# Three blocks for even tokens ahead of the odd ones, and the merges' weights transposed later and stored from another queue

## The chip, the cores and the metric

The kernel runs on one core of one Trainium2 chip. A core has TensorE (PE, with its weight loads shown apart as PEld), VectorE (DVE), ScalarE (ACT), GpSimd (POOL) and SyncE (SP). Each has its own queue of instructions and works it off in order; they wait for one another by semaphores. Transfers between the core's memory and DRAM are issued from such a queue too, here nearly all from SP's and some from GpSimd's, and run on 16 DMA engines. The metric is the time of one execution on the device, in microseconds.

## The reference

The kernel computes one hybrid decoder block over 1024 tokens of width 1024 in float32. In short:

```
h = rms_norm(x, g_pre_mix);  z = h @ w_in
q, k, v, glu_in, z_ga, z_gc = split(z)
# attention: 3 groups (dilations 1, 4, 16) of 8 heads of 64, a banded window of 128 steps
o_g, lse_g = dilated_group_attention(q_g, k_g, v_g, bias_g, window_g, dilation_g)
alpha  = softmax(stack(lse_g), axis=groups)
y_attn = (sum_g alpha_g * o_g) @ w_attn_out
# convolution: gated unit -> causal depthwise conv of 31 taps -> layer norm -> swish -> projection
u = silu(layer_norm(causal_depthwise_conv(u_in * sigmoid(gate)) + b_dw))
y_conv = u @ w_conv_out + b_conv_out
merged = sigmoid(z_ga) * y_attn + sigmoid(z_gc) * y_conv
x = x + rms_norm(merged @ w_mix_out)
x = x + rms_norm(swiglu_ffn(rms_norm(x)))
```

Two places matter here. One is `u @ w_conv_out`, the convolution's projection. The other is `alpha`, by which the three groups' attention outputs are merged, head by head and token by token.

## The kernel before, in words

A product of float32 matrices is done as three matmuls of rounded parts: every operand is split into a high part (a cast on ACT) and a low part (the remainder, a subtraction on DVE or GpSimd). A unit of such a product is a block of 128 output columns for 512 tokens: eight steps of 128 in depth, three matmuls each (lines 305, 307, 309), 24 matmuls into one PSUM bank.

The program writes the order of every engine's instructions out by hand. The main loop issues matmuls. After each step of depth (three matmuls) `tick` is called, which advances background generators: a generator's `yield n` lets n further ticks pass before it goes on. After each single matmul `beat` is called, which advances attention (the generator `fine`) at a set rate of steps per matmul. So "some steps later" means some ticks later, and where an instruction stands in its engine's queue follows from the ticks, not from time.

The part around the change is the stage in which attention's last steps run beside the convolution's projection. At its start stands the last gate projection; then come 16 units of the convolution's projection: 8 blocks of output columns n, each for the even tokens (hf = 0) and for the odd tokens (hf = 1). Per unit:

- `B.weights(co[n])`, called at the unit for even tokens, makes sure that the weights of block n are split, loads those of block n + 2 from SP's queue (line 177) and queues the split of block n + 1, in two halves, one each few ticks (line 188 on ACT, 189 on DVE). A load of the gate values of block n + 1 follows on SP (line 1569).
- `B.unit` does the 24 matmuls. Its right-hand operands come from `conv_split`, a background generator that loads the normalised convolution output and splits it in 16 pieces, first eight for even tokens, then eight for odd ones (line 1242 on ACT, 1243 on DVE). When a unit asks for a piece that is not there yet, the generator is advanced at that point.
- Line 1586 on DVE adds the bias and multiplies by the gate, which frees the PSUM bank; the result is stored by SP some ticks later (line 1588).

The units stand in the order (n, hf) = (0, even), (1, even), (0, odd), (1, odd), (2, even), (2, odd), (3, even) and so on.

Attention itself does scores (line 1049, with the bias and a running minimum on DVE, line 1052), exponentials (1062 on ACT), transposes of the probabilities (1087, copied by ACT on 1094 and split by DVE on 1095), and the products with the values (1122), whose outputs DVE copies (1142).

For each of four head pairs (hp = 0 to 3) a `merge` runs as a background generator when that pair's last group is done. It computes the merge weights alpha on DVE (lines 1170 to 1177, with one exponential on ACT, 1172) in one small tile `mrg`, of which there is a single buffer for all four merges. PE transposes the weights (1183), ACT copies them from PSUM (1184), SP stores them to DRAM (1188). From there they are loaded back spread over partitions (`spread`, line 1158), beside the attention outputs (line 1197), and DVE multiplies and adds (1211, 1215, 1220, 1225, 1230). The result is split (195, 196) and is the operand of attention's output projection, which comes after the 16 units.

While attention runs, PSUM has two banks for units (tag g), two for scores, two for transposes, two for attention's outputs. Once all four merges have done their transpose (`B.weighed == 4`) the next unit to begin switches to six banks for units.

Of the kernel before, what the change touches and what calls it, by code (L numbers as in the profile page):

```python
# [62 lines left out]
class Build:  # L63
# [1098 lines left out]
    def merge(self, hp, st, last):  # L1162

        nc = self.nc
        yield 2
        t = self.tiny(128, "mrg", 1)
        m, r = (t[:, i * 16:(i + 1) * 16].rearrange("p (u e) -> p u e", u=8) for i in range(2))
        w = t[:, 32:80].rearrange("p (g u e) -> p g u e", g=3, u=8)
        low, tot = st[:, :, :, 0:2], st[:, :, :, 2:4]
        nc.vector.tensor_reduce(m, low.rearrange("p g u e -> p u e g"), AX.X, OP.min)  # L1170
        nc.vector.tensor_tensor(w, low, m.unsqueeze(1).to_broadcast([128, 3, 8, 2]), op=OP.subtract)
        nc.scalar.activation(t[:, 32:80], t[:, 32:80], AF.Exp, scale=-1.0)
        yield 2
        nc.vector.tensor_tensor(tot, tot, w, op=OP.mult)
        nc.vector.tensor_reduce(m, tot.rearrange("p g u e -> p u e g"), AX.X, OP.add)
        nc.vector.reciprocal(r, m)
        nc.vector.tensor_tensor(t[:, 80:].rearrange("p (g e u) -> p g u e", g=3, e=2).rearrange("p g u e -> p g u e"), w,
                                r.unsqueeze(1).to_broadcast([128, 3, 8, 2]), op=OP.mult)
        yield 1
        m = r = w = low = tot = None  # L1180
        yield 3
        ps = self.bank("t")
        nc.tensor.transpose(ps[0:48, :128], t[:, 80:], self.ident)
        nc.scalar.copy(t[0:48], ps[0:48, :128])
        ps = None
        self.weighed += 1
        yield 1
        nc.sync.dma_start(self.d_w[hp].rearrange("f (u p) -> (f u) p", u=8), t[0:48])
        t = None
        yield 4  # L1190

        while not self.ending or hp > self.turn:
            yield 0

        def load(g):
            y = self.slot()
            nc.sync.dma_start(y, self.d_att[g, hp])
            return y

        y = load(0)  # L1200
        yield 1
        x = self.spread(hp, 0)
        yield 1
        z = load(1)
        yield 1
        w = self.spread(hp, 1)
        yield 7
        self.turn += hp == 0
        while self.fine is not None or hp > self.done:
            yield 0  # L1210
        nc.vector.tensor_tensor(y, y, x, op=OP.mult)
        x = None
        x = self.spread(hp, 2)
        yield 1
        nc.vector.tensor_tensor(z, z, w, op=OP.mult)
        w = None
        w = load(2) if last is None else last
        last = None
        yield 1
        nc.vector.tensor_tensor(y, y, z, op=OP.add)  # L1220
        z = None
        self.turn += hp > 0
        yield 9
        self.done += 1
        nc.vector.tensor_tensor(w, w, x, op=OP.mult)
        x = None
        yield 2

        z = self.slot()
        nc.vector.tensor_tensor(z.rearrange("p (m c) -> p c m", c=8), *(a.rearrange("p (c m) -> p c m", c=8) for a in (y, w)),  # L1230
                                op=OP.add)
        y = w = None
        yield 2
        self.OT[hp] = self.both(z)
# [166 lines left out]
def build(ctx, tc, aps):  # L1401
    B = Build(ctx, tc, aps)
    nc = B.nc
# [150 lines left out]
    def conv_rhs(hf):  # L1554
        def at(kt):
            while len(B.cop[hf]) <= kt:
                next(cs[0][0])
            x = B.cop[hf][kt]
            return x[:, :H], x[:, H:]
        return at  # L1560
# [3 lines left out]
    def gate_load(d, late=0):  # L1564
        c = B.slot()
        if late:
            B.later(late, lambda: nc.sync.dma_start(c, d))
        else:
            nc.sync.dma_start(c, d)
        return c  # L1570
# [1 line left out]
    nxt = gate_load(B.d_gc[0], 1)  # L1572
    ws = {}

    for n, hf in [(0, 0), (1, 0), (0, 1), (1, 1)] + [(n, hf) for n in range(2, 8) for hf in range(2)]:
        if hf == 0:
            ws[n] = B.weights(co[n])
            mg[n] = nxt
            nxt = gate_load(B.d_gc[n + 1]) if n < 7 else (gate_load(B.d_ga[0]), gate_load(B.d_gc[0]))
        if B.tags["g"] == 2 and B.weighed == 4:  # L1580
            B.banks(g=6, s=2)
        ps = B.unit(ws[n], conv_rhs(hf), KT)
        c = mg[n].rearrange("p (m e) -> p e m", e=2)[:, hf]
        if n >= 8 - LATE - EARLY:
            nc.scalar.activation(c, c, AF.Sigmoid)
        nc.vector.scalar_tensor_tensor(c, ps, B.col(C_BCO + n), c, op0=OP.add, op1=OP.mult)
        if hf:
            B.later(9, lambda n=n: nc.sync.dma_start(B.d_gc[n], mg.pop(n)))
            c = None
            del ws[n]  # L1590
# [210 lines left out]
    for j in range(PLAIN, FT):  # L1801
        s = [None, None]
        p, odd = divmod(j, 2)
# [105 lines left out]
    for i in range(7):  # L1909
# [12 lines left out]
        n = NP - LAST if i == 6 else NP  # L1922
# [112 lines left out]
```

## Time and profile before

| | |
|---|---|
| median of 3 runs | 1714.13 us (1712.32 to 1714.29) |
| profiled execution | 1711.05 us |
| its span in the trace | 1709.1 us |
| PE, DVE, ACT, POOL busy | 99%, 73%, 46%, 28% |
| granted TensorE clock | 0.999 |

The profile is of one execution. The span runs from the first to the last instruction, and the execution's own time is some 2 us longer. Busy time of an engine is the sum of its instructions' durations. Matmuls overlap one another, so that a matmul of 512 columns has a duration of 0.39 us, while in an undisturbed row of them one starts every 0.227 us. In a view of instructions in order, the first number is the start in us from the span's start, the second the duration; a bracket at the end of a row gives the idle time of the engine before it and the instruction that ended it. In a view of waits the numbers are the total in us, the times, and the longest. In a view of transfers, KB are those of one and the last number is the median time from issue to landing.

### The profile page before, as it was taken

What the parts mean: (1) busy time and instruction counts of PE and PEld (TensorE: products, weight loads), DVE (VectorE), ACT (ScalarE), POOL (GpSimd) and SP (SyncE); (2) the same over time, 40 slices, a digit from 0 to 9 for tenths busy, and PEclk for the clock granted to TensorE, in tenths of its full rate; (3) what the DMA queues carried; (4) which work ended last, traced back from release to release, by engine and by line L of the source; (5) the groups of instructions that cost most, each with busy time, mean ns of one, the idle gap of its engine ahead of it and who ended that gap; (6) DMA issues with size and microseconds to landing.
All of it is one profiled execution on the core that took longest, in us unless ns stands there. A gap on an engine that the chain in (4) does not pass through costs nothing.

```text
span 1709.1 us, 24547 instructions
## 1 busy us (share of the span) xinstructions
PE 1692.4 (99%) x8758; PEld 1437.4 (84%) x8758; DVE 1251.2 (73%) x2214; ACT 790.1 (46%) x1550; POOL 474.5 (28%) x383
## 2 busy tenths in 40 slices
PE   8999999999999999999999999999999999999998
PEld 7788888888888999999878888888888888888886
DVE  6789988888998667677885855775566556677686
ACT  6344344434444576677722436633333333354463
POOL 0017777887886124544300210000000000000000
PEclk9999999999999999999999999999999999999999
DMA  4352433455668887878998722123222322494234
GB/s 166 103 185 87 148 124 129 155 195 174 173 166 204 249 261 211 233 200 238 296 275 285 265 74 99 68 99 124 93 92 105 118 93 92 145 375 146 100 135 154
DMA packets 162422, 283.43 MB, mean 166 GB/s; under 512 B 47249, under 2 KB 78796, under 8 KB 162300
## 3 DMA queue, kind: packets, MB, share of 16 engines
q1 hardware_dynamic: 160204, 275.98, 50.8%
q0 software_dynamic: 1808, 5.61, 0.9%
q8 instruction: 69, 1.13, 0.3%
q14 instruction: 53, 0.43, 0.1%
q10 hardware_dynamic: 288, 0.27, 0.0%
HBM read 191.10 MB, written 95.42 MB: 168 GB/s over the span
## 4 chain that ended last, share of the span: by engine, by line
PE 95%; ACT 1%; issue 1%; DVE 1%; POOL 1%; DMA 1%; SPq 0%; DVEq 0%; ACTq 0%; POOLq 0%
PE p L321 16%; PE p L323 16%; PE p L322 16%; PE p L1919 12%; PE p L1648 5%; PE p L305 5%; PE p L307 5%; PE p L309 5%; PE p L1122 3%; PE p L948 2%; PE p L950 2%; PE p L952 2%; PE p L1049 2%; PE p L556 2%; PE p L1087 2%
## 5 line engine op out<-in xcount | busy, mean ns | idle before, releaser
L321 PE MATMUL p<-b,b 128*128 128x512 f32 x1204 | 468.6, 389 | 0.3 <-ACT c L340 0.3
L323 PE MATMUL p<-b,b 128*128 128x512 f32 x1204 | 468.4, 389 | 0.0
L322 PE MATMUL p<-b,b 128*128 128x512 f32 x1204 | 468.4, 389 | 0.0
L321 PEld LDWEIGHTS p<-b,b 128*128 128x128 f32 x1204 | 226.0, 188 | 47.8 <-ACT c L340 0.7
L322 PEld LDWEIGHTS p<-b,b 128*128 128x128 f32 x1204 | 226.0, 188 | 47.1
L323 PEld LDWEIGHTS p<-b,b 128*128 128x128 f32 x1204 | 226.0, 188 | 47.0
L1919 PE MATMUL p<-b,b 128*128 128x512 f32 x924 | 209.6, 389 | 0.0
L1919 PEld LDWEIGHTS p<-b,b 128*128 128x128 f32 x924 | 173.4, 188 | 36.0
L686 DVE SCALAR_TENSOR_TENSOR p<-b,par,p 128x511 f32<-128x511 f32 (+14 forms) x232 | 163.5, 739 | 0.0
L305 PE MATMUL p<-b,b 128*128 128x512 f32 x368 | 146.7, 399 | 1.3 <-ACT b L1242 1.2
L307 PE MATMUL p<-b,b 128*128 128x512 f32 x368 | 145.6, 396 | 0.0
L309 PE MATMUL p<-b,b 128*128 128x512 f32 x368 | 145.6, 396 | 0.0
L195 ACT CAST b<-d 128x1024 fp32r<-128x1024 f32 x86 | 90.4, 1051 | 105.1 <-POOL d L216 55.1
L196 POOL TENSOR_TENSOR b<-d,b 128x1024 fp32r<-128x1024 f32 x44 | 106.8, 2428 | 79.8 <-ACT b L195 72.4
L196 DVE TENSOR_TENSOR b<-d,b 128x1024 fp32r<-128x1024 f32 x42 | 51.3, 1222 | 101.0 <-ACT b L195 101.0
L948 PE MATMUL p<-b,b 128*128 128x256 f32 x384 | 112.8, 294 | 0.0
L952 PE MATMUL p<-b,b 128*128 128x256 f32 x384 | 112.2, 292 | 0.0
L950 PE MATMUL p<-b,b 128*128 128x256 f32 x384 | 112.2, 292 | 0.0
L1243 DVE TENSOR_TENSOR b<-b,b 128x512 fp32r<-128x512 f32 x133 | 91.7, 693 | 22.0 <-ACT b L1242 20.2
L1242 ACT CAST b<-b 128x512 fp32r<-128x512 f32 x133 | 82.1, 619 | 46.8 <-PE p L1919 18.1
L1648 PE MATMUL p<-b,b 128*128 128x512 f32 x384 | 89.4, 391 | 0.0
L195 ACT CAST b<-b 128x1024 fp32r<-128x1024 f32 x47 | 49.4, 1052 | 80.8 <-POOL b L223 37.2
(234 smaller groups left out, 3035.3 us busy)
## 6 DMA issues: line engine op xcount, KB each, us to landing
b<-w_in SPq DMA_DIRECT2D x30, 512.0 KB, 4.9
dk<-c SPq DMA_DIRECT2D x48, 256.0 KB, 2.9
dq<-c SPq DMA_DIRECT2D x48, 256.0 KB, 3.5
b<-dq SPq DMA_DIRECT2D x48, 256.0 KB, 4.3
b<-dk SPq DMA_DIRECT2D x48, 256.0 KB, 8.1
b<-w_fi SPq DMA_DIRECT2D x24, 512.0 KB, 4.8
d<-w_in SPq DMA_DIRECT2D x23, 512.0 KB, 4.8
dqS<-c SPq DMA_DIRECT2D x44, 256.0 KB, 2.2
```

What stands on the lines that cost most here:

```text
L196: self.wsplit.tensor_tensor(lo, x, f(hi), op=OP.subtract)
L305: nc.tensor.matmul(ps, hi[:, s], a, start=kt == 0, stop=False)
L307: nc.tensor.matmul(ps, hi[:, s], b, start=False, stop=False)
L309: nc.tensor.matmul(ps, lo[:, s], a, start=False, stop=kt == nk - 1)
L321: nc.tensor.matmul(ps, hi[:, s], a, start=first and kt == 0, stop=False, skip_group_check=True)
L322: nc.tensor.matmul(ps, hi[:, s], b, start=False, stop=False, skip_group_check=True)
L323: nc.tensor.matmul(ps, lo[:, s], a, start=False, stop=kt == 3, skip_group_check=True)
L686: nc.vector.scalar_tensor_tensor(A[i][:, j:], src[i][:, :H - j], w[i], A[i][:, j:], op0=OP.mult, op1=OP.add)
L948: nc.tensor.matmul(o, a, hi[:, s], start=kt == 0, stop=False)
L950: nc.tensor.matmul(o, a, lo[:, s], start=False, stop=False)
L1648: nc.tensor.matmul(banks[tt][nh], st, wt[:, nh * H:(nh + 1) * H], start=bool(kt == 0 and a), stop=bool(kt == KT - 1 and b))
L1919: nc.tensor.matmul(acc[t], x, y, start=first and e == 0, stop=last and e == 2, skip_group_check=True)
```

## The change

Three edits, all in the stage described above.

The units of the convolution's projection now stand in the order (0, even), (1, even), (2, even), (0, odd), (1, odd), (2, odd), (3, even), (3, odd) and so on. What is called at a unit for even tokens moves with it: the load of block 4's weights, the load of block 3's gate values and the split of block 3's weights now stand at the third unit instead of the fifth.

In each merge, PE's transpose comes five ticks after the weights' last step instead of three; in the last merge (hp = 3) eight. Everything behind it in that merge is moved by as much.

The transposed weights are stored from GpSimd's queue instead of SP's.

In PE's order, the first two transposes move behind some 26 other instructions, the third behind 11, the fourth behind 15 matmuls, which is out of the unit (2, odd) and into (3, even). The number of instructions on PE, ACT and DVE is the same.

```diff
@@ merge(self, hp, st, last)
         yield 1
         m = r = w = low = tot = None
-        yield 3
+        yield 5 + 3 * (hp > 2)
         ps = self.bank("t")
         nc.tensor.transpose(ps[0:48, :128], t[:, 80:], self.ident)
         nc.scalar.copy(t[0:48], ps[0:48, :128])
         ps = None
         self.weighed += 1
         yield 1
-        nc.sync.dma_start(self.d_w[hp].rearrange("f (u p) -> (f u) p", u=8), t[0:48])
+        nc.gpsimd.dma_start(self.d_w[hp].rearrange("f (u p) -> (f u) p", u=8), t[0:48])
         t = None
         yield 4
@@ build(ctx, tc, aps)
-    for n, hf in [(0, 0), (1, 0), (0, 1), (1, 1)] + [(n, hf) for n in range(2, 8) for hf in range(2)]:
+    for n, hf in [(n, hf) for hf in range(2) for n in range(3)] + [(n, hf) for n in range(3, 8) for hf in range(2)]:
         if hf == 0:
             ws[n] = B.weights(co[n])
             mg[n] = nxt
```

## The prediction

> **What bounds the kernel now.** I read the page first: the busy shares and the chain that ended last.
>
> ```profile
> span 1709.1 us, 24547 instructions
> PE 1692.4 (99%) x8758; PEld 1437.4 (84%) x8758; DVE 1251.2 (73%) x2214; ACT 790.1 (46%) x1550; POOL 474.5 (28%) x383
> PE 95%; ACT 1%; issue 1%; DVE 1%; POOL 1%; DMA 1%; SPq 0%; DVEq 0%; ACTq 0%; POOLq 0%
> ```
>
> TensorE is busy 1692.4 of 1709.1 us, so the whole kernel has 16.7 us without it, and an edit that neither adds nor removes a matmul can win only from that. Next, the view of waits for PE alone, and the busy time by stretches around the edited code (start and end of a stretch, its length, then busy time and instructions of PE, PEld, DVE, ACT, POOL, clock, DMA share, GB/s).
>
> ```profile
> PE p L305 <- ACT b L1242: 1.2, 1, 1.2
> PE p L1183 <- DVE mrg L1177: 1.2, 1, 1.2
> 841.50:854.10 12.60, 11.20 (x80) 8.98 (x79) 9.38 (x36) 8.46 (x31) 2.12 (x4) 1.00 1.05 240
> 868.50:875.50 7.00, 5.78 (x26) 4.46 (x25) 5.99 (x12) 1.54 (x4) 0.00 (x0) 1.00 0.34 105
> ```
>
> Two of PE's few waits lie on lines that the change moves. The first is the convolution's first block for odd tokens waiting for its own operands (L1242 is the rounding half of a split, L1243 the remainder). The second is the last merge's transpose (L1183) waiting for its weights (L1177), with PE's later matmuls queued behind it. The DMA share of 0.34 in the second stretch, where the first has 1.05, shows another thing: SP is standing still there.
>
> **Stall one, in PE's own rows.** Matmuls overlap, so I price a stall by the distance between starts.
>
> ```profile
> 829.72 0.48 PE L305 MATMUL p<-b,b 128*128 128x512 f32 x1
> ...
> 834.76 0.58 PE L1122 MATMUL p<-c,b 128*66 128x128 f32 x3
> ...
> 840.04 0.34 PE L1122 MATMUL p<-c,b 128*66 128x128 f32 x3
> ...
> 841.19 0.39 PE L305 MATMUL p<-b,b 128*128 128x512 f32 x1
> 841.42 0.38 PE L1087 MATMUL p<-ident,c 128*128 128x128 f32 x2
> 841.55 0.48 PE L307 MATMUL p<-b,b 128*128 128x512 f32 x1
> ...
> 849.24 0.34 PE L1122 MATMUL p<-c,b 128*66 128x128 f32 x3
> 849.68 0.50 PE L305 MATMUL p<-b,b 128*128 128x512 f32 x1
> ...
> 850.98 0.38 PE L1087 MATMUL p<-ident,c 128*128 128x128 f32 x2
> 852.60 0.49 PE L305 MATMUL p<-b,b 128*128 128x512 f32 x1 [1.25 <-ACT b L1242]
> 852.93 0.34 PE L1122 MATMUL p<-c,b 128*66 128x128 f32 x3
> 853.33 0.50 PE L307 MATMUL p<-b,b 128*128 128x512 f32 x1
> 854.13 0.40 PE L305 MATMUL p<-b,b 128*128 128x512 f32 x1
> ```
>
> 841.19 starts block 0 for odd tokens, 854.13 the next. A transpose pair is normally followed after 0.13 us (841.42 to 841.55); here after 1.62 (850.98 to 852.60): 1.49 lost. The L1122 group takes 0.16 (0.34 with an overlap of 0.18) and is here followed after 0.44 (849.24) and 0.40 (852.93), against some 0.18: 0.26 and 0.22 lost. Together 2.0 us. A cruder price: this block lasted 12.94 (841.19 to 854.13), the one before it 11.47 (829.72 to 841.19): 1.5. I take 2.0, with 1.5 as the lower end.
>
> In the change, block 2 for even tokens stands in this place and block 0 for odd tokens starts one block later. The last split on ACT begins at
>
> ```profile
> 851.93 0.62 ACT L1242 CAST b<-b 128x512 fp32r<-128x512 f32 x1
> ```
>
> and its remainder is there when PE's L307 at 853.33 takes it. It is paced by the same ticks in the new order, and the earliest that the last operand is used is then seven eighths into a block that begins near 852, that is about 860. Stall one goes whole: **-2.0**.
>
> **What takes its place.** Weights of block 3 are now split during this block instead of during the fifth: two halves, each an ACT cast (L188) and a DVE subtraction (L189), in among the attention's exponentials and copies. DVE had 9.38 of 12.60 there; 1.2 more is about 10.6 in some 11: tight. The nearest case is the block from 829.72, which carried block 2's halves: there one L1122 group was stretched to 0.58 (834.76) against 0.34 (840.04). So between 0 and 0.25, and I take **+0.15**, nearer the upper end because DVE is no emptier here. The weights must also be there:
>
> ```profile
> 833.48 0.43 SPq L177 DMA_DIRECT2D b<-w_co  x1
> DMA to landing us min/median/max: 8.0/9.8/11.6
> ```
>
> Block 3's load is issued at 833.48, in its old place on SP, so it lands at 843.3 (841.5 to 845.1); the first L188 now stands on ACT at about 844.4. The median clears it by 1.1 us, the slowest misses it by 0.7. An attention copy has about a microsecond before its L1122 group needs it, so even this costs a few tenths.
>
> On SP the load of block 4 and a gate load move ahead of one spread of the first merge and the statistics loads: 1 MB earlier by some 14 us and three more buffers held meanwhile. Those spreads are used only after attention ends (about 863), so this is priced at nothing; if that cover goes, DVE's merge steps wait, and what they feed is priced below.
>
> **Stall two, from store to transpose.** The chain view and then DVE's, PE's rows.
>
> ```profile
> 862.40 5.86 DMA dw<-mrg
> ```
>
> ```profile
> 868.38 0.23 DVE L1170 TENSOR_REDUCE mrg<-stat 128x16 f32<-128x48 f32 x1 [0.93 <-DMA dw<-mrg]
> 868.64 0.21 DVE L1171 TENSOR_TENSOR mrg<-stat,mrg 128x48 f32<-128x48 f32 x1
> 869.72 0.69 DVE L189 TENSOR_TENSOR b<-b,b 128x512 fp32r<-128x512 f32 x1 [0.87 <-ACT b L188]
> 870.33 1.22 DVE L1220 TENSOR_TENSOR b<-b,b 128x1024 f32<-128x1024 f32 x1
> ...
> 872.25 0.24 DVE L1177 TENSOR_TENSOR mrg<-mrg 128x48 f32<-128x48 f32 x1
> 872.38 0.74 DVE L1586 SCALAR_TENSOR_TENSOR b<-p,par,b 128x512 f32<-128x512 f32 x1
> ```
>
> ```profile
> 861.76 0.27 PE L1183 MATMUL p<-ident,mrg 128*48 128x128 f32 x1
> ...
> 863.52 0.40 PE L309 MATMUL p<-b,b 128*128 128x512 f32 x1
> ...
> 871.03 0.39 PE L309 MATMUL p<-b,b 128*128 128x512 f32 x1
> 872.64 0.27 PE L1183 MATMUL p<-ident,mrg 128*48 128x128 f32 x1 [1.22 <-DVE mrg L1177]
> ...
> 875.52 0.39 PE L305 MATMUL p<-b,b 128*128 128x512 f32 x1
> ...
> 929.92 0.39 PE L305 MATMUL p<-b,b 128*128 128x512 f32 x1
> ```
>
> The merges share one small tile, so merge 3 may not write it (L1170) until merge 2's store has read it: 5.86 us in a full DMA stage. DVE then does L1171, a weight half, L1220 and the reciprocal steps; L1177 ends at 872.49, PE starts at 872.64, where 871.26 was due: **1.4 us** lost.
>
> In the change merge 2's transpose comes 11 PE instructions later, behind the matmul at 863.52, so near 863.75; with stall one gone, near 861.9. Transpose to issue took 0.64 us on SP's way (861.76 to 862.40); the same puts GpSimd's issue at 862.5 to 862.6, hardly later than before. Merge 3's transpose moves 15 matmuls on, into the next block (block 3, even), one step in. That block starts at 875.52 - 1.85 - 1.4 = 872.3, the transpose is due at 873.0.
>
> Landing on GpSimd's queue has no row for this store. Bounds: the nearest stores from that queue, 512 KB in 2.9 to 7.6, and 16 KB in small pieces in up to 7.8.
>
> ```profile
> DMA to landing us min/median/max: 2.9/4.9/7.6
> dst<-stat POOLq DMA_DIRECT2D x2, 16.0 KB, 7.8
> ```
>
> I take 5, the large store's median, because this store has 512-byte rows and not 16-byte pieces: landed at 867.6. From L1170 to the end of L1586 DVE took 4.74 (868.38 to 873.12), of which 1.48 were the weight half (868.85 to 870.33) that has moved to the third block. So L1177 ends 2.5 and L1586 3.3 after landing: 870.1 and 870.9. The transpose due at 873.0 no longer waits: **-1.4**.
>
> There is a new deadline. PE's bank set changes from two to six output banks only when all four merges are transposed, looked at when a block begins; before, that was block 3 even, now it is block 3 odd. So block 3 even must reuse the bank that the L1586 above frees, by 872.3. It is free at 870.9: 1.4 us of room, cost nothing; with 7.8 to land it is 1.4 late.
>
> On GpSimd nothing waits behind the last two stores, since its next instruction is far off; the first two fall where GpSimd, 28% busy over the span, has nothing ahead but another small store. On SP the wait of merge 3's store, with a datt load, a weight load and a gate load queued behind it, is gone.
>
> ```profile
> 920.03 0.95 POOL L189 TENSOR_TENSOR b<-b,b 128x256 fp32r<-128x256 f32 x1 [75.06 <-ACT b L188]
> 915.08 1.23 DVE L196 TENSOR_TENSOR b<-b,b 128x1024 fp32r<-128x1024 f32 x1 [0.66 <-ACT b L195]
> ```
>
> Later on, attention's output projection starts at 929.92 and its last operand is split by 916.31 (915.08 + 1.23): 13.6 us of room, from which the gain takes 3 and merge 3's later steps at most 3.4 (15 matmuls of 0.227). No new wait.
>
> **Sum.** -2.0 + 0.15 - 1.4 = -3.25 us. The profiled execution took 1711.05 us (span 1709.1), so 1707.8; it stood 3.1 below the median of the three runs, 1714.13 (1712.32 to 1714.29), which makes 1710.9, 0.19% less. What this kernel's measurement tells from no change is about 0.2%, 3.4 us, so the forecast lies on the border.
>
> **Rivals.** *A: both stalls go*, gain 2.1 to 4.3 (1.5 - 0.25 + 0.9 to the full 3.5 plus scatter): 1710.9, chance 0.64, of which I put 0.34 beyond 0.2% and 0.30 within.
>
> *B: the store lands late, and the bank takes the transpose's place.* Over 6.4 us from issue to landing the block at 872.3 waits; at 7.8, for 1.4 us: gain 1.85, 1712.3. For it: the small store's 7.8. Against: it is in 16-byte pieces. The Trainium skill, "DMA: Bandwidth & Descriptors", section "Issuing engines are not separate DMA queues", speaks against the change here: DMAs of all engines share the same 16 DMA engines, and another issuing engine saves only the time to issue. By that rule the store would still take the 5.86 of the row, land at 868.5 and free the bank at 871.8, 0.5 before it is due: the same sum, with a third of the room. No row here shows one store from both queues. Chance 0.12, within 0.2%.
>
> *C: slower.* Block 3's weight half waits on ACT for its load, with the attention's exponentials and copies queued behind it, and these hold PE. Each microsecond beyond about one of room costs one. To lose the gain and 3.4 us more it needs to land 6.7 later than 845.4, 18.6 after its issue, where the slowest row has 11.6. For it: DMA share 1.05 in this stage, and 1 MB newly ahead on the rings. There it gives 1717.5, and at 20 us 1719. Chance 0.12, also for what else a tight third block may do.
>
> *D: the waits only move* (the splits for odd tokens are late again a block on, or merge 3's chain follows its transpose): 1714.1, chance 0.04. Against it speak the 8 us and 2.9 us of room above.
>
> *E: more than forecast*, 4.3 to 6: SP's freed time fills the stretch with the 0.34 share, and small losses elsewhere go too: 1709. Chance 0.08; against it PE was already full from 875.5 on.
>
> Faster by over 0.2%: 0.34 + 0.08 = 0.42. Within: 0.30 + 0.12 + 0.04 = 0.46. Slower: 0.12. A alone spans 1709.8 to 1712.0; with B, D, part of E and the scatter of the runs (1 us each way) the range is 1708.8 to 1714.5; it leaves out C and half of E.
>
> **What would show it.** Right: no PE wait on L1242 between 840 and 865, none on L1177; the two gaps of 1.62 and 1.61 gone; block 3 even starting near 872.3; SP moving between 867 and 873. Wrong: PE's wait on L1586 at block 3 even (B), ACT's L188 waiting for the weight load near 844 (C), L1242 on PE's list again (D).

## The result, and the profile after

The changed kernel is slower: 1717.75 us median of 7 runs (1714.78 to 1720.12), against 1712.32 (1710.68 to 1717.15) for the kernel before run beside it, a ratio of 1.0028 with a 95% interval of [1.0015, 1.0041] (taken over all runs; the two medians alone give 1.0032). Its profiled execution took 1718.57 us, 7.5 more than the one before. The page of the kernel after, its first lines and the chain that ended last:

```profile
span 1716.6 us, 24557 instructions
PE 1694.1 (99%) x8758; PEld 1438.3 (84%) x8758; DVE 1251.2 (73%) x2214; ACT 789.6 (46%) x1550; POOL 476.9 (28%) x387
PE 52%; issue 2%; DMA 2%; DVE 1%; ACT 0%; POOL 0%; DVEq 0%; SPq 0%; ACTq 0%; POOLq 0%
```

PE has the same 8758 matmuls; its busy time rose by 1.7 us (1692.4 to 1694.1), so some matmuls ran slower, and the other 5.8 us of the longer span are PE standing still. Where it stands is told by the view of waits for PE:

```profile
PE p L1122 <- ACT c L1094: 5.2, 1, 5.2
PE p L1049 <- DMA b<-dk: 1.4, 1, 1.4
```

The two waits that the change was forecast to remove, on L1242 and on L1177, are gone from the list. A single wait of 5.2 us has come in their place, on a line that the change does not touch: attention's product with the values (L1122), waiting for the copied probabilities (L1094). Its surroundings in time order, first GpSimd and PE:

```profile
747.33 0.61 POOL L887 CAST b<-b 64x512 fp32r<-64x512 f32 x1
747.89 0.54 POOL L1188 DMA_DIRECT2D dw<-mrg  x1
...
751.08 0.28 PE L950 MATMUL p<-b,b 128*128 128x256 f32 x1
756.54 1.20 PE L1122 MATMUL p<-c,b 128*66 128x256 f32 x3 [5.18 <-ACT c L1094]
757.54 0.41 PE L952 MATMUL p<-b,b 128*128 128x256 f32 x1
757.76 0.41 PE L948 MATMUL p<-b,b 128*128 128x256 f32 x1
...
760.21 0.29 PE L950 MATMUL p<-b,b 128*128 128x256 f32 x1
```

then DVE and ACT of the same stretch:

```profile
749.09 0.09 DVE L1052 DVE_READ_ACCUMULATOR2_ANT stat<- 128x1 f32 x1
755.22 0.22 DVE L1170 TENSOR_REDUCE mrg<-stat 128x16 f32<-128x48 f32 x1 [6.05 <-issue]
...
755.77 0.24 ACT L1172 ACTIVATE mrg<-mrg 128x48 f32<-128x48 f32 x1 [8.11 <-DVE mrg L1171]
755.92 0.57 ACT L1094 CAST c<-p 128x512 fp32r<-128x512 f32 x1
```

and the same spot before (transposition, store and the next merge's first instruction, with the store's landing from the view of transfers), followed by the landing after:

```profile
742.19 0.27 PE L1183 MATMUL p<-ident,mrg 128*48 128x128 f32 x1
...
742.86 0.32 SPq L1188 DMA_DIRECT2D dw<-mrg  x1
...
748.84 0.22 DVE L1170 TENSOR_REDUCE mrg<-stat 128x16 f32<-128x48 f32 x1
...
dw<-mrg SPq DMA_DIRECT2D x1, 24.0 KB, 1.9
```

```profile
dw<-mrg POOLq DMA_DIRECT2D x1, 24.0 KB, 7.3
```

Read together: merge 1 begins 6.65 us after merge 0's transpose (742.19 to 748.84 before), in the same tile. Before, merge 0's store had read the tile at 744.8 (742.86 + 1.9), 4.1 us before L1170 came. After, the store is issued 5.03 us later than before (747.89 against 742.86) and takes 7.3 us to land instead of 1.9: done at 755.2, 10.4 us later. That is 6.3 more than the 4.1 of room, and L1170 begins at 755.22 with DVE idle for 6.05 ahead of it. The profile says "issue" there, since it names no releaser; the time of the landing names it. ACT's exponential L1172 needs L1171, and the copy L1094 that PE wants is queued right behind L1172. So the chain runs from store to DVE to ACT to PE, and attention, which has nothing to do with the merge, waits in three queues.

Why the store goes late and lands late is told by the rows of GpSimd and SP. Before, GpSimd works off eight casts of keys in a row, with attention's store among them, and SP issues the loads of the next queries and keys (2 MB) only behind the merge's store:

```profile
742.05 0.61 POOL L886 CAST b<-b 64x512 fp32r<-64x512 f32 x1
...
744.62 0.56 POOL L1149 DMA_DIRECT2D datt<-d  x1
...
747.24 0.61 POOL L887 CAST b<-b 64x512 fp32r<-64x512 f32 x1
```

```profile
744.25 0.58 SPq L870 DMA_DIRECT2D b<-dq  x1
...
747.22 2.60 SPq L877 DMA_DIRECT2D b<-dk  x4
```

After, the merge's store stands behind those casts on GpSimd, and SP, no longer held by it, issues the same loads some three microseconds sooner, nearly all ahead of it:

```profile
740.89 0.68 SPq L870 DMA_DIRECT2D b<-dq  x1
...
744.51 3.81 SPq L877 DMA_DIRECT2D b<-dk  x4
```

So the two landings do not differ by the queue alone. The DMA share was 0.51 in the 1.9 us of the store before (742.86 to 744.76); after, it was 1.08 from 747 to 748, and 0.99 or more in every microsecond until 753.

The stall costs more than its 5.2 us. By stretches around it (busy time and instructions of PE, PEld, DVE, ACT, POOL, then the granted clock, DMA share, GB/s), the kernel after:

```profile
752.00:754.00 2.00, 0.00 (x0) 0.00 (x0) 0.00 (x0) 0.00 (x0) 0.00 (x0) 0.80 0.98 307
...
758.00:759.00 1.00, 1.00 (x7) 1.00 (x7) 0.96 (x3) 0.00 (x0) 0.70 (x1) 0.50 0.00 0
...
760.00:761.00 1.00, 1.00 (x11) 1.00 (x10) 0.95 (x3) 0.44 (x3) 0.00 (x0) 0.99 0.00 0
```

The granted clock fell during the stall (a mean of 0.80 from 752 to 754), stayed at 0.50 and came back at 760, some 3.5 us after PE began again; the matmuls of 256 columns start every 0.22 us there (757.54 to 757.76), where 0.12 is usual. By PE's starts, the stall lost 5.34 us (5.46 from 751.08 to 756.54, less the usual 0.12). The instructions behind it took 3.67 us (756.54 to 760.21), and the same ones 1.89 before (751.13 to 753.02), so another 1.8 were lost: 7.1 together. The wait for keys (L1049, 1.4 us) is the only other new loss above half a microsecond.

### The profile page after: what moved, and what is told of

It reads as the page before. It is cut to its first block, busy times and chain, and to the rows that moved or that the text cites. A ratio compares the mean times of both kernels' runs of the same rounds, so it can differ in the third digit from the quotient of the medians.

```text
span 1716.6 us, 24557 instructions
## 1 busy us (share of the span) xinstructions
PE 1694.1 (99%) x8758; PEld 1438.3 (84%) x8758; DVE 1251.2 (73%) x2214; ACT 789.6 (46%) x1550; POOL 476.9 (28%) x387
## 4 chain that ended last, share of the span: by engine, by line
PE 52%; issue 2%; DMA 2%; DVE 1%; ACT 0%; POOL 0%; DVEq 0%; SPq 0%; ACTq 0%; POOLq 0%
PE p L1919 12%; PE p L321 7%; PE p L322 7%; PE p L323 7%; PE p L1648 5%; PE p L305 3%; PE p L309 3%; PE p L307 3%; PE p L1122 1%; PE p L1049 1%; DMA b<-w_co 1%; PE p L1087 1%; DMA dgc<-b 0%; DMA b<-dact 0%; PE p L952 0%
## 5 line engine op out<-in xcount | busy, mean ns | idle before, releaser
L1242 ACT CAST b<-b 128x512 fp32r<-128x512 f32 x133 | 82.1, 619 | 48.1 <-PE p L1919 18.3
L1122 PE MATMUL p<-c,b 128*66 128x128 f32 (+1 forms) x620 | 87.2, 242 | 6.3 <-ACT c L1094 5.2
```

## The experiments

Theory one: the loss is merge 0's store, which goes late from GpSimd's queue and lands late, while merge 1 has to wait for it because all merges share one tile. Its rivals: two, the new order of the blocks costs more than it wins; three, GpSimd's own time for issuing, or its packets among the others, slow everything down. The first four kernels were run side by side with the kernel before (median 1713.53 us, 27 runs), the last four too, on another chip (1714.38 us, 27 runs); each ratio is against the kernel before beside it.

**Stores back on SP.** The changed kernel with one word undone:

```diff
-        nc.gpsimd.dma_start(self.d_w[hp]....., t[0:48])
+        nc.sync.dma_start(self.d_w[hp]....., t[0:48])
```

> The changed kernel with the stores of the merges' weights back on SP's queue; block order and delays as changed. Theory one (the store lands late on GpSimd's queue, and the one tile of the merges makes DVE wait for it in the second merge): that wait of 6 us on L1170 near 749 shrinks below 1.5 us, since SP's store landed in 1.9 us there, and the kernel gains 5 to 9 us on the changed one, so it ends 1 to 4 us below the kernel before. Rival two (the new order of blocks, with weights split and loaded earlier, costs the time): it stays 4 to 5 us above the kernel before.

Measured: 1710.97 us, ratio 0.9985 [0.9974, 0.9997]. L1170 begins at 749.00 with no wait, and the 5.2 us are gone. The queue is what turns the gain into a loss. What is left of the old second stall has moved, as rows of DVE and PE show:

```profile
872.02 0.23 DVE L1170 TENSOR_REDUCE mrg<-stat 128x16 f32<-128x48 f32 x1 [4.76 <-DMA dw<-mrg]
874.46 0.74 DVE L1586 SCALAR_TENSOR_TENSOR b<-p,par,b 128x512 f32<-128x512 f32 x1
...
875.25 0.50 PE L305 MATMUL p<-b,b 128*128 128x512 f32 x1 [0.61 <-DVE b L1586]
876.05 0.27 PE L1183 MATMUL p<-ident,mrg 128*48 128x128 f32 x1
```

Merge 2's store, issued by SP at 864.78, holds L1170 until 872.02; the transpose no longer waits, but the bank that L1586 frees does, for 0.61 us.

**GpSimd's queue, each store from a place of its own.** The changed kernel, with the copy out of PSUM put into unused columns of another tile:

```diff
-        nc.scalar.copy(t[0:48], ps[0:48, :128])
+        t = None
+        s = self.par[0:48, hp % 2 * 128:hp % 2 * 128 + 128]
+        nc.scalar.copy(s, ps[0:48, :128])
...
-        nc.gpsimd.dma_start(self.d_w[hp]....., t[0:48])
+        nc.gpsimd.dma_start(self.d_w[hp]....., s)
```

> The changed kernel, all three edits kept and the stores on GpSimd's queue, but the transposed weights are copied from PSUM into columns of the parameter tile that are no longer used, two places by turns, so that no store is read from the merges' tile. Theory one: no DVE wait for the store is left, the 5.3 us on PE and the slow matmuls behind it go, and the kernel ends 3 to 5 us below the kernel before, at a ratio of 0.997 to 0.999. Rival three (GpSimd's own time on issuing the stores, or the stores' packets, hold up attention): the wait goes but PE still stands for some us near 751, and it stays 3 to 5 us above.

Measured: 1709.82 us, ratio 0.9982 [0.9973, 0.9991]. GpSimd's and DVE's rows, and the transfer:

```profile
747.90 0.53 POOL L1190 DMA_DIRECT2D dw<-par  x1
...
749.11 0.22 DVE L1170 TENSOR_REDUCE mrg<-stat 128x16 f32<-128x48 f32 x1
...
865.95 0.22 DVE L1170 TENSOR_REDUCE mrg<-stat 128x16 f32<-128x48 f32 x1
...
dw<-par POOLq DMA_DIRECT2D x1, 24.0 KB, 6.3
```

The first store is issued just as late as in the changed kernel (747.90 against 747.89), from the same queue, and lands at 754.2; L1170 has long gone by then (749.11), and nobody waits. So GpSimd's time and packets cost nothing that can be measured: rival three falls. A late landing costs only because the tile is needed again.

**The block order alone.** The kernel before with the one line of the loop:

```diff
-    for n, hf in [(0, 0), (1, 0), (0, 1), (1, 1)] + [(n, hf) for n in range(2, 8) for hf in range(2)]:
+    for n, hf in [(n, hf) for hf in range(2) for n in range(3)] + [(n, hf) for n in range(3, 8) for hf in range(2)]:
```

> The kernel before with the new order of blocks alone. Theory one: the first stall (2.0 us, on L1242) goes and nothing takes its place but 0.2 to 0.4; the second stall, on L1177, shrinks from 1.4 to between 0 and 1.4, since a half of block 3's split has left its chain: 1.5 to 3.5 us below the kernel before. Rival two: 4 to 5 us above it, with PE waiting in the third block.

Measured: 1712.11 us, ratio 0.9988 [0.9979, 0.9997]: rival two falls, the order wins. The first stall is gone; the second, which was expected to shrink, grew. Its rows:

```profile
869.50 0.23 DVE L1170 TENSOR_REDUCE mrg<-stat 128x16 f32<-128x48 f32 x1 [3.79 <-DMA dw<-mrg]
...
872.19 0.27 PE L1183 MATMUL p<-ident,mrg 128*48 128x128 f32 x1 [1.94 <-DVE mrg L1177]
...
873.46 0.62 PE L309 MATMUL p<-b,b 128*128 128x512 f32 x1
...
876.86 0.40 PE L307 MATMUL p<-b,b 128*128 128x512 f32 x1
```

Issued by SP at 861.26, the store lets L1170 go only at 869.50. PE waits 1.94 us, and from 873.46 to 876.86 eight matmuls of 512 columns take 3.40 us, 0.425 each instead of 0.227, another 1.6 us.

**The queue alone.** The kernel before with the one word, at its old place in the ticks:

```diff
-        nc.sync.dma_start(self.d_w[hp]....., t[0:48])
+        nc.gpsimd.dma_start(self.d_w[hp]....., t[0:48])
```

> The kernel before with GpSimd's queue for the stores alone. Theory one: the first merge's store is issued near 748, behind GpSimd's copies, and lands 4 to 7 us later, so L1170 of the second merge waits 3 to 6 us, PE nearly as long, and the last merge's transpose is no earlier than before: 4 to 8 us above the kernel before. Rival two: within 1.5 us of it.

Measured: 1721.33 us, ratio 1.0051 [1.0039, 1.0064]. GpSimd and DVE:

```profile
748.35 0.53 POOL L1188 DMA_DIRECT2D dw<-mrg  x1
...
755.60 0.22 DVE L1170 TENSOR_REDUCE mrg<-stat 128x16 f32<-128x48 f32 x1 [6.15 <-DMA dw<-mrg]
```

Here the releaser is named. Merge 0 is transposed at 742.72, and yet its store goes at 748.35, behind six casts of keys (L886, L887) and attention's store: the old early place in the ticks buys nothing, because GpSimd's queue sets the time. The one word alone is worse than the whole change, and at the upper edge of what was expected (7.8 us by the medians, 8.7 by the ratio): it has nearly the same wait (5.1 us), the stall on L1242 is still there with 1.2 us, a wait for keys (L1049) takes 1.9, and the granted clock is halved behind all three (last section).

**The later transposes alone.** The kernel before with the one `yield`:

```diff
-        yield 3
+        yield 5 + 3 * (hp > 2)
```

> The kernel before with the later transposes alone: stores on SP, blocks in their old order. It computes the whole reference. Theory one (the loss is the late landing of merge 0's store on GpSimd's queue, with merge 1 right behind it in the one tile): no wait at merge 1, since SP's store there landed in 1.9 us. Stall one stays (1.25 us of PE waiting for L1242, 2.0 in all). Stall two goes or shrinks, because merge 3's transpose is due some four steps later: between 0 and -1.4, ratio 0.9990 to 1.0002. If the later transposes by themselves cost something in the first two merges, which the first four runs do not exclude, the ratio is above 1.0005 and PE's lost time near 751 is over 1 us.

Measured: 1712.66 us, ratio 0.9995 [0.9984, 1.0006], no difference that can be told. L1170 of merge 1 starts at 749.84 without a wait. The first stall stays, the second is gone (the last transpose, at 879.03, has no wait), and this profiled execution has a wait for keys, and a halved clock soon after it, that the one of the kernel before has not:

```profile
PE p L1049 <- DMA b<-dk: 1.4, 1, 1.4
PE p L305 <- ACT b L1242: 1.2, 1, 1.2
```

**Only the last two stores from GpSimd's queue.** The changed kernel, the first two merges' stores on SP:

```diff
-        nc.gpsimd.dma_start(self.d_w[hp]....., t[0:48])
+        (nc.gpsimd if hp > 1 else nc.sync).dma_start(self.d_w[hp]....., t[0:48])
```

> The changed kernel, with only the last two merges' stores on GpSimd's queue and the first two on SP. It computes the whole reference. Theory one: PE's 5 us wait near 751 and the half-speed matmuls behind it go, and the two stalls of the kernel before are gone as forecast, so 2 to 3.5 us under the kernel before, ratio 0.9980 to 0.9990; what is left is a short wait at merge 3 of under 0.5 us for merge 2's store. If the loss was spread over all four stores, the ratio stays above 1.0000.

Measured: 1710.90 us, ratio 0.9982 [0.9970, 0.9993]. PE's waits in the edited part are a short one for the bank and a 0.9 at L1049:

```profile
PE p L1049 <- issue: 0.9, 1, 0.9
...
PE p L305 <- DVE b L1586: 0.3, 1, 0.3
```

So the first two stores carry the whole loss, and by the rows of the changed kernel merge 0's alone, since nobody waits for merge 1's (merge 2's L1170 starts at 859.77 without a wait): with them, 1.0028; without them, 0.9982. That is 0.46%, 7.9 us of 1714, where PE's rows gave 7.1.

**The order, with stores on SP from their own place.** The old delays, the new order, and the store as in the second experiment, on SP:

```diff
+        s = self.par[0:48, hp % 2 * 128:hp % 2 * 128 + 128]
+        nc.scalar.copy(s, ps[0:48, :128])
...
+        nc.sync.dma_start(self.d_w[hp]....., s)
...
+    for n, hf in [(n, hf) for hf in range(2) for n in range(3)] + [(n, hf) for n in range(3, 8) for hf in range(2)]:
```

> The new block order, the old delays, stores on SP, but each store reads a place of its own (columns of another tile) so that the next merge need not wait for it. It computes the whole reference. Theory one's second half (one tile for all merges): the wait of L1170 for the store goes, and with it the 1.9 us that PE's transpose waited in the order-alone run and the half-speed matmuls behind it. What is left of that wait is DVE's weight half and L1220 ahead of the reciprocal steps: 0 to 0.7 us. Ratio 0.9970 to 0.9982 against the kernel before. If the transpose waited for DVE's other work and not for the store, the wait stays above 1 us and the ratio is 0.9985 or more.

Measured: 1709.69 us, ratio 0.9972 [0.9962, 0.9983], faster than both kernels. DVE and PE at the last merge:

```profile
865.19 0.22 DVE L1170 TENSOR_REDUCE mrg<-stat 128x16 f32<-128x48 f32 x1
...
867.49 0.25 DVE L1177 TENSOR_TENSOR mrg<-mrg 128x48 f32<-128x48 f32 x1
...
869.66 0.27 PE L1183 MATMUL p<-ident,mrg 128*48 128x128 f32 x1
```

L1177 ends 1.9 us before PE transposes, without any later transpose and without GpSimd's queue. The second stall was the tile, not DVE's other work.

**The changed kernel, on SP from own places.** As the one before, with the new delays too:

```diff
+        yield 5 + 3 * (hp > 2)
```

> The changed kernel with stores on SP and from a place of their own. It computes the whole reference. Theory one: neither queue nor tile makes anyone wait, the bank wait of the SP run (0.6 us at L305 for L1586) goes as well, so 0.5 to 1 us under that run: ratio 0.9972 to 0.9983. If the queue still mattered once the tile is free, it would differ from the run with own places on GpSimd's queue (0.9982) by more than 0.001; theory one expects less.

Measured: 1709.48 us, ratio 0.9974 [0.9962, 0.9985]. It cannot be told from the one before, so the later transposes are worth nothing that these runs can tell once the tile is free; nor, with certainty, from the same kernel on GpSimd's queue (0.9982 [0.9973, 0.9991]): the difference of 0.0008 is within both intervals.

## Why the prediction was wrong

The forecast was 1710.9 us, 0.19% less than before, in a range up to 1714.5; the result is 0.28% more.

**The step that failed** is the one that costs the first two merges' stores at nothing: "the first two fall where GpSimd, 28% busy over the span, has nothing ahead but another small store". Four things in it were wrong. GpSimd's share of the whole span says nothing of that place: the rows of the kernel before show eight casts of 0.61 us there (742.05 to 747.85), and attention's store among them is of 512 KB, not small. After, three of these casts begin behind the transpose, and the store goes 2.4 us after it (745.52 to 747.89) where SP took 0.67. The landing was 7.3 us; the prediction had asked for a landing on that queue only for merge 2's store, and had allowed 5 to 7.8 there. It saw that SP is freed where merge 3's store waited, but not that the same happens at merge 0, where the freed SP fills the DMA engines just ahead of the store. And it had named the rule that a merge may not write the tile before the store has read it, and applied it to merges 2 and 3 alone. Merge 1 follows merge 0 by 6.65 us, as closely as merge 3 follows merge 2 (transpose at 861.76, L1170 at 868.38). Before, the 1.9 us landing on SP left 4.1 us of room, so no wait was to be seen at merge 1, and the prediction looked for the change's cost only where waits already stood. Applied to merge 0, its own 0.64 us to the issue and 5 to 7.8 us to the landing, from the transpose at 745.52, give a store done between 751.2 and 754.0. With L1170 due at about 749.2 that is a wait of 2 to 4.8 us on DVE. PE lost 0.7 us less than DVE waited (5.34 against 6.05), so by these terms 1.3 to 4.1 us of the forecast gain of 3.25 were at stake, before any matmul runs slower. None of the rivals held this case. The slower one, C, names 1717.5 us, close to the 1717.75 measured, but by luck: its mechanism, the weight half on ACT, did not come.

Point by point, for the rest:

- *Stall one goes whole, -2.0*: right. L1242 is not on PE's list after, nor in any kernel with the new order; it stays, at 1.2 us, in both kernels with the old one (the queue alone, the delays alone).
- *Weights of block 3 in the third block, +0.15*: nothing measurable. Block 2 for even tokens took 10.8 us (850.71 to 861.50) with no distance of PE more than 0.09 us above the usual; rival C has no trace.
- *Stall two goes, -1.4*: right in place, a little small in what follows. Rows of POOL, DVE and PE after:

```profile
872.40 0.55 POOL L1188 DMA_DIRECT2D dw<-mrg  x1 [16.98 <-ACT mrg L1184]
...
878.85 0.22 DVE L1170 TENSOR_REDUCE mrg<-stat 128x16 f32<-128x48 f32 x1 [4.23 <-issue]
...
881.28 0.74 DVE L1586 SCALAR_TENSOR_TENSOR b<-p,par,b 128x512 f32<-128x512 f32 x1
...
882.88 0.27 PE L1183 MATMUL p<-ident,mrg 128*48 128x128 f32 x1
```

  From issue to L1170 are 6.45 us, where 5 was taken. The transpose does not wait, but L1586 ends at 882.02 and PE loses 0.3 us at 881.6 to 882.1 for its bank. That is rival B at its threshold of 6.4 us, in small. The Trainium skill, "DMA: Bandwidth & Descriptors", section "Issuing engines are not separate DMA queues", says that the transfers of all engines run on the same 16 DMA engines and interleave. In this stage the runs agree, for from SP the same store held L1170 for 7.2 us after its issue (864.78 to 872.02) and for 8.2 in the order-alone kernel (861.26 to 869.50). At merge 0 SP was much quicker: 1.9 us before, and with the later transpose at most 2.4 (SP's issue at 746.60, L1170 free to go at 749.00), against 7.3 on GpSimd's queue. But there the DMA engines were not equally full: the share was 0.51 and 0.58 over those two stretches, and about 1 around the store from GpSimd's queue, with SP's loads now ahead of it. That the loads and not the queue make the difference is argued from this, not shown: every kernel with merge 0's store on GpSimd's queue has both.
- *The sum, -3.25*: where the first two stores are left on SP, the kernel is 0.18% faster [0.07%, 0.30%], 3.1 us. The mechanisms that were costed had the right sign and, within that interval, the right sum; the one that was not costed took 7 to 8 us. That 3.1 comes so near 3.25 is in part luck: that kernel's profiled execution still has the 0.9 us at L1049 and the 0.3 for the bank.

Open is the wait for keys (L1049). It shows in the profiled execution of the changed kernel and of six of the eight others, at 0.5 to 1.9 us, and not in the one before (in two of them the view names no releaser). The order-alone kernel issues these loads within about a microsecond of where the kernel before does (817.21 and 820.17 against 818.25 and 820.79) and still has it; the two fastest kernels lack it. Whether it is more than the scatter of a landing in a full stage was not tried.

## What to carry to other kernels

When a transfer is moved to another queue, cost every transfer that the line issues, each at its own place: what stands ahead of it on the new queue there, how long it lands there, and how soon its source is written again. A place without a wait is not a place with room: take the margin (here 4.1 us) from the rows and hold the new delay against it. Ask also what the old queue will issue sooner once the transfer is gone from it. And where a store holds a tile that the next step needs, a source of its own for the store took the wait away on either queue (0.9982 on GpSimd's, 0.9972 and 0.9974 on SP's) and made its queue and its time matter no more than these runs can tell.

## What the runs showed of the hardware that was not expected

A stall of PE can have a second price behind it. After the 5.2 us wait the granted clock was 0.50 until 760, and 1.8 us more were lost; after the 1.94 us wait of the order-alone kernel it was 0.50 from about 873.5 to 876.9, and 1.6 us were lost, nearly as much as the wait. That kernel's stretch in the middle:

```profile
874.00:875.00 1.00, 1.00 (x4) 0.81 (x3) 1.00 (x2) 0.00 (x0) 0.00 (x0) 0.50 0.72 201
```

The queue-alone kernel shows it after its waits of 5.1 and 1.87 us, and once after one of 1.25 (the stall on L1242):

```profile
865.00:866.00 1.00, 1.00 (x8) 0.80 (x6) 0.00 (x0) 0.04 (x1) 0.00 (x0) 0.50 1.05 254
```

The delays-alone kernel shows it after its 1.42 us for keys, which a wait of 0.46 us followed 1.5 us later:

```profile
839.00:840.00 1.00, 1.00 (x6) 0.90 (x5) 0.67 (x2) 1.00 (x4) 0.00 (x0) 0.50 1.04 369
```

But the same wait on L1242 (1.25 us before, 1.24 in the delays-alone kernel) left the clock at 1.00, and so did the 1.22 us on L1177 before and the 1.39 us for keys in the changed kernel. So the length of a wait does not by itself tell whether the clock falls: among the waits of 1.22 to 1.42 us it did twice and did not four times, and from 1.87 us on it did each time (four waits). What decides in between was not tried. Added up from the granted clock of each microsecond, the half clock lasted about 3.4 us in four cases and about 6.8 us around the two long stalls. PE lost half of the time that it worked in it: 1.5 to 1.8 us, and 2.6 behind the long stall of the queue-alone kernel, where PE worked through 5.2 us of it (756.91 to about 762.1).

The Trainium skill, "TensorE: Matmul & The Clock Gate", "Part 1: The HAM clock gate", says that the clock is either full or half, and that it halves after at least one idle window of about 3.4 us and is back after about as long busy. The runs agree on the half, and on the way back where PE worked throughout (873.46 to 876.86, 3.40 us); the idle time that was enough here was shorter, 1.9 us and in one case 1.25.

The scatter of the runs goes with this clock. Of the 27 runs of the kernel before beside the first four experiments, the 14 with a mean clock of 0.999 took 1712.6 us on average, the 8 with 0.998 took 1715.5 and the 3 with 0.997 took 1716.4 (the remaining two, at 1.000, took 1713.2). So it seems that half clocks come and go in the kernel before too, and that its profiled execution, at 0.999, shows one of the quicker cases. No profile of one at 0.997 was taken.
